# Gate values placed by two products of the rounded type, and weight halves made by a casting DMA

## Chip, cores and metric

The kernel runs on one core of a Trainium2 chip. The metric is the device time of one execution in microseconds; a kernel is timed by the median of several runs.

## What is computed

Two transformer blocks on one sequence of 256 positions of width 1024, all in float32. The change lies in the last part of the second block, a mixture of 16384 small experts (`peer_ffn`). For each position, eight heads score 2 x 128 keys, take the 16 best of each half, combine them into 256 candidates, take the 16 best of these, and turn their scores into 16 gates by a softmax. An expert's number is 128 i + j, where i comes from one half and j from the other. The block's output is the sum over the 128 picked experts of gate x gelu(u . x) x v.

```
sv, si = lax.top_k(s, PEER_TOPK)
cand_idx = (si[:, :, 0, :, None] * PEER_NKEYS + si[:, :, 1, None, :]).reshape(...)
best, pick = lax.top_k(cand, PEER_TOPK)
expert_idx = jnp.take_along_axis(cand_idx, pick, axis=-1)
gates = jax.nn.softmax(best, axis=-1)
...
u = expert_u[ic]
hval = jnp.einsum('cd,chkd->chk', xc, u).astype(jnp.float32)
a = (gc * jax.nn.gelu(hval, approximate=False)).astype(xc.dtype)
return jnp.einsum('chk,chkd->cd', a, expert_v[ic])
```

## The kernel before

**The dense form.** The kernel gathers nothing. It computes u . x for all 16384 experts, applies gelu, multiplies by a gate matrix that is zero wherever an expert was not picked, and multiplies by all of v. The matrix is `GT` [128, 128, 256]: j on the partitions, then i, then the position t. The first linear part (`linear(..., P, 8, evu)`) fills `GT` with gelu(u . x) in pairs of i; the last part (L1550, L1559) multiplies by v.

**Weights.** Each matrix product is done in three products of a rounded type (`float32r`, FR in the code), for which weights and inputs are split into a rounded half and a remainder. `unit()` makes one weight tile of 128 x 1024: SyncE issues the load of `raw` (L202), ScalarE writes the rounded half `whi` (L206), VectorE (or GpSimd, where `pool_k` is set) subtracts and writes `wlo` (L209). `raw`, `whi` and `wlo` have three buffers each; `take(2)` keeps two tiles ahead of the one in use. TensorE then runs 24 products of 256 columns with a tile, three (L231, L232, L233) for each of its eight 128 x 128 blocks. One tile of the first linear part serves one i.

**Gates.** `topk` finds i, j and the gate for each position on VectorE, in two rounds of 128 positions, and transposes them into `it["i"]`, `it["j"]`, `it["g"]` (tiles ti, tj, tg), so that a position's 128 picks lie along the partitions. When both rounds are done, `wstep()` starts: 64 steps of four positions each, run beside the first linear part. A step has two halves. `build` (VectorE, then ScalarE) writes two one-hot matrices per position: `oe`, which lies in `xres` (L1468), for i, and `oj` (L1469) for j, and ScalarE multiplies `oe` by the gate into `om` (L1471, one instruction per position). `place`, one step later, multiplies the two on TensorE (L1478, four products in plain float32, each 128 columns wide), which gives the position's 128 x 128 gate matrix in PSUM. What is there of gelu by then (the first `i1` values of i) is multiplied by it on VectorE (L1481), the rest of the gates is copied into `GT` by ScalarE (L1483). Where gelu comes later, `evu` writes it (L1454) or multiplies it in (L1457 on ScalarE and L1458 on VectorE). `oj` and `om` have two buffers each.

**Order.** `linear` calls `tick` after each tile; the steps run at a rate of 1.75 per pair of tiles, so most tiles are followed by one step. The instruction order on each engine is then settled by the tile framework when the program is built; an engine takes its instructions strictly in that order.

Of the kernel before, what the change touches and what calls it, by code (L numbers as in the profile page):

```python
# [8 lines left out]
FT = mybir.dt.float32  # L9
FR = mybir.dt.float32r  # L10
# [3 lines left out]
AF = mybir.ActivationFunctionType  # L14
OP = mybir.AluOpType
# [3 lines left out]
P = 128  # L19
S = 256  # L20
# [142 lines left out]
class Kernel:  # L163
    def __init__(self, ctx, tc, A, out):
        self.ctx, self.tc, self.A, self.out = ctx, tc, A, out
        self.nc = tc.nc
        nc = self.nc
        self.cst = ctx.enter_context(tc.tile_pool(name="cst", bufs=1))
        self.wp = ctx.enter_context(tc.tile_pool(name="wp", bufs=2))
        self.unit_i = 0  # L170
        self.ahead = []
        self.pos = 0
        self.bg = []
        self.pool_k = 0
        self.soon = []
        self.acc_bufs = 2
        self.vec = self.cst.tile([P, A["vec"].shape[1]], FT, name="vec")
        nc.sync.dma_start(self.vec, A["vec"])
        self.main = self.cst.tile([P, 3, P], FT, name="main")
        self.ident, self.ones, self.iota = (self.main[:, i, :] for i in range(3))  # L180
        self.eps = self.cst.tile([P, 3], FT, name="eps")
        for i, e in enumerate((EPS, LN_EPS, LNX_EPS)):
            nc.gpsimd.memset(self.eps[:, i:i + 1], e)
        self.mod = self.cst.tile([P, 48], FT, name="mod")
        self.junk = self.cst.tile([P, 1], FT, name="junk")
        self.hx = [self.cst.tile([P, 8, S + 2], FR, name=n) for n in ("hh", "hl")]
        self.hh, self.hl = (h[:, :, :S] for h in self.hx)
        self.r1 = self.cst.tile([P, 4], FT, name="r1")
        self.gm = self.cst.tile([P, 8], FT, name="gm")
        self.g2 = self.cst.tile([P, 8], FT, name="g2")  # L190
# [8 lines left out]
    def unit(self):  # L199
        nc = self.nc  # L200
        raw = self.raw()
        nc.sync.dma_start(raw, self.A["wts"][self.unit_i])  # L202
        self.unit_i += 1
        hi = self.wp.tile([P, 8, P], FR, name="whi", bufs=3)
        lo = self.wp.tile([P, 8, P], FR, name="wlo", bufs=3)
        nc.scalar.activation(hi, raw, AF.Copy)  # L206
        c = 8 - self.pool_k
        if c:
            nc.vector.tensor_tensor(lo[:, :c], raw[:, :c], hi[:, :c].bitcast(FT), op=OP.subtract)  # L209
        if c < 8:  # L210
            nc.gpsimd.tensor_tensor(lo[:, c:], raw[:, c:], hi[:, c:].bitcast(FT), op=OP.subtract)  # L211
        return hi, lo
# [1205 lines left out]
    def peer(self):  # L1418
        nc, tc = self.nc, self.tc
        V, SC, G, T = nc.vector, nc.scalar, nc.gpsimd, nc.tensor  # L1420
        x = self.xres
        with ExitStack() as es:
            pk = es.enter_context(tc.tile_pool(name="pk", bufs=1))
            it = {n: pk.tile([P, S], FT, name="t" + n) for n in ("i", "j", "g")}
            GT = pk.tile([P, P, S], FT, name="GT")
            with ExitStack() as e2:
                dp = e2.enter_context(tc.tile_pool(name="dp", bufs=1, space=bass.MemoryType.DRAM))
# [33 lines left out]
                io4 = self.iota[:, None, :].to_broadcast([P, 4, P])  # L1461

                def build(t0):
                    oj = pw.tile([P, 4, P], FT, name="oj")
                    om = pw.tile([P, 4, P], FT, name="om")
                    oe = wide[2 + t0 // 4 % 2].rearrange("p a (b c) -> p (a b) c", b=2)
                    z = slice(t0, t0 + 4)
                    V.tensor_tensor(oe, io4, it["i"][:, z, None].to_broadcast([P, 4, P]), op=OP.is_equal)  # L1468
                    V.tensor_tensor(oj, io4, it["j"][:, z, None].to_broadcast([P, 4, P]), op=OP.is_equal)  # L1469
                    for j in range(4):  # L1470
                        SC.activation(om[:, j, :], oe[:, j, :], AF.Copy, scale=it["g"][:, t0 + j:t0 + j + 1])  # L1471
                    return t0, oj, om

                def place(t0, oj, om):
                    i1 = st["u"]
                    wps = psum.tile([P, 4, P], FT, name="ax")
                    for j in range(4):
                        T.matmul(wps[:, j, :], oj[:, j, :], om[:, j, :], start=True, stop=True)  # L1478
                    z = slice(t0, t0 + 4)
                    if i1:  # L1480
                        V.tensor_tensor(Gv[:, z, :i1], Gv[:, z, :i1], wps[:, :, :i1], op=OP.mult)  # L1481
                    if i1 < P:
                        SC.activation(Gv[:, z, i1:], wps[:, :, i1:], AF.Copy)  # L1483
                    st["n"] = t0 + 4
# [12 lines left out]
                def start_w():  # L1497
                    for _ in top():
                        yield
                    self.pool_k = 0  # L1500
                    self.spawn(wstep(), 1.75)

                self.pool_k = 8
# [10 lines left out]
                                                     op=OP.subtract)  # L1514

                self.linear(psum, hh, hl, P, 8, evu, outer=True)
                self.drain()
                es5.close()
                po = e2.enter_context(tc.tile_pool(name="po", bufs=2))
# [59 lines left out]
    def topk(self, psum, qh, keys, scr, it, st):  # L1579
# [36 lines left out]
        for t in range(2):  # L1616
# [55 lines left out]
            T.transpose(tp[:, 1, :], res[:, 1].rearrange("p h k -> p (h k)"), self.ident)  # L1672
            T.transpose(tp[:, 2, :], e.rearrange("p h k -> p (h k)"), self.ident)
            z = slice(t * P, (t + 1) * P)
            for i, n in enumerate("ijg"):
                SC.activation(it[n][:, z], tp[:, i, :], AF.Copy)
            yield

    def build(self):
# [25 lines left out]
```

## Time and profile before

| what | value |
|---|---|
| median of three runs | 1557.8 us (1556.55 to 1558.47) |
| the profiled execution, its own time | 1556.54 us |
| its span, first to last instruction | 1554.8 us |
| share of the span in which TensorE is busy | 97% |
| VectorE, ScalarE, GpSimd | 73%, 54%, 22% |
| first product of a step, last product of a step | 923.2 us, 1185.3 us |
| data moved | 279.67 MB, mean 180 GB/s |

The page names TensorE as the engine that is nearly always at work, but a busy share is an average over stages. What matters for the change is the stretch from about 906 us, when the gates are found, to 1197 us, when the first linear part is over. In the rows below PE is a product on TensorE, PEld the weight load that goes with each product, DVE is VectorE, ACT ScalarE, POOL GpSimd, SP SyncE. A product's duration includes its way through the array, so two products overlap: the pace is read from the distance of their starts.

### The profile page before, as it was taken

What the parts mean: (1) busy time and instruction counts of PE and PEld (TensorE: products, weight loads), DVE (VectorE), ACT (ScalarE), POOL (GpSimd) and SP (SyncE); (2) the same over time, 40 slices, a digit from 0 to 9 for tenths busy, and PEclk for the clock granted to TensorE, in tenths of its full rate; (3) what the DMA queues carried; (4) which work ended last, traced back from release to release, by engine and by line L of the source; (5) the groups of instructions that cost most, each with busy time, mean ns of one, the idle gap of its engine ahead of it and who ended that gap; (6) DMA issues with size and microseconds to landing.
All of it is one profiled execution on the core that took longest, in us unless ns stands there. A gap on an engine that the chain in (4) does not pass through costs nothing.

```text
span 1554.8 us, 28988 instructions
## 1 busy us (share of the span) xinstructions
PE 1510.4 (97%) x11494; PEld 1409.9 (91%) x11494; DVE 1130.5 (73%) x1811; ACT 839.1 (54%) x1400; POOL 335.9 (22%) x301
## 2 busy tenths in 40 slices
PE   6898999999999999999999999999999999999998
PEld 5797889999999999999999999999999888888886
DVE  7789976787656677667689968889997555555555
ACT  4563334666644365544445457777775445454444
POOL 7614644325500100025790600000000000000000
PEclk9899999999999999999999999999999999999999
DMA  9445557476565644447456564444445665666664
GB/s 365 153 157 166 175 164 230 150 257 198 172 198 182 201 150 142 144 150 229 151 177 190 163 190 136 150 149 137 150 149 174 207 208 184 193 197 191 192 196 127
DMA packets 75449, 279.67 MB, mean 180 GB/s; under 512 B 8369, under 2 KB 9009, under 8 KB 73649
## 3 DMA queue, kind: packets, MB, share of 16 engines
q1 hardware_dynamic: 75312, 277.82, 56.1%
q8 instruction: 90, 1.47, 0.4%
q14 instruction: 47, 0.38, 0.1%
HBM read 275.69 MB, written 2.10 MB: 179 GB/s over the span
## 4 chain that ended last, share of the span: by engine, by line
PE 46%; DVE 2%; POOL 1%; issue 1%; ACT 0%; DVEq 0%
PE ax L1550 22%; PE mm L233 7%; PE mm L232 7%; PE mm L231 7%; PE ax L1478 4%; POOL wlo L211 1%; POOL GT L1627 0%; DVE GT L1659 0%; DVE GT L1566 0%; DVE GT L1657 0%; DVE wlo L209 0%; PE ax L1600 0%; DVE GT L1568 0%; DVE GT L1637 0%; DVE GT L1638 0%
## 5 line engine op out<-in xcount | busy, mean ns | idle before, releaser
L206 ACT ACTIVATE whi<-raw 128x1024 fp32r<-128x1024 f32 x453 | 478.6, 1058 | 535.8 <-PE mm L232 205.5
L209 DVE TENSOR_TENSOR wlo<-raw,whi 128x1024 fp32r<-128x1024 f32 (+2 forms) x413 | 496.3, 1204 | 265.0 <-ACT whi L206 264.4
L231 PE MATMUL mm<-hh,whi 128*128 128x256 f32 x1816 | 523.8, 288 | 3.7 <-ACT gate L581 2.5
L233 PE MATMUL mm<-hh,wlo 128*128 128x256 f32 x1816 | 514.9, 284 | 3.2 <-DVE wlo L209 2.3
L232 PE MATMUL mm<-hl,whi 128*128 128x256 f32 x1816 | 512.0, 282 | 1.1 <-DVE hl L1513 0.7
L231 PEld LDWEIGHTS mm<-hh,whi 128*128 128x128 f32 x1816 | 344.0, 189 | 9.5 <-issue 4.7
L233 PEld LDWEIGHTS mm<-hh,wlo 128*128 128x128 f32 x1816 | 344.8, 190 | 5.1 <-DVE wlo L209 2.7
L232 PEld LDWEIGHTS mm<-hl,whi 128*128 128x128 f32 x1816 | 345.2, 190 | 2.9 <-issue 1.4
L211 POOL TENSOR_TENSOR wlo<-raw,whi 128x256 fp32r<-128x256 f32 (+2 forms) x112 | 187.9, 1684 | 159.9 <-ACT whi L206 99.9
L1550 PE MATMUL ax<-whi,ah 128*128 128x512 f32 x504 | 155.6, 390 | 0.0
L1550 PE MATMUL ax<-whi,al 128*128 128x512 f32 x504 | 155.3, 389 | 0.0
L1550 PE MATMUL ax<-wlo,ah 128*128 128x512 f32 x504 | 155.1, 389 | 0.0
L1550 PEld LDWEIGHTS ax<-whi,al 128*128 128x128 f32 x504 | 94.6, 188 | 19.8
L1550 PEld LDWEIGHTS ax<-wlo,ah 128*128 128x128 f32 x504 | 94.6, 188 | 19.7
L1550 PEld LDWEIGHTS ax<-whi,ah 128*128 128x128 f32 x504 | 94.2, 188 | 19.2
L1471 ACT ACTIVATE om<-xres,tg 128x128 f32<-128x128 f32 x256 | 85.2, 391 | 1.0 <-DVE xres L1468 1.0
L233 PE MATMUL ax<-hh,wlo 128*128 128x258 f32 x256 | 72.9, 285 | 1.3 <-DVE wlo L209 1.3
L1481 DVE TENSOR_TENSOR GT<-GT,ax 128x208 f32<-128x208 f32 (+31 forms) x64 | 62.4, 974 | 16.1 <-PE ax L1478 15.9
L231 PE MATMUL ax<-hh,whi 128*128 128x258 f32 x256 | 72.7, 284 | 0.0
L232 PE MATMUL ax<-hl,whi 128*128 128x258 f32 x256 | 72.2, 282 | 0.0
L231 PE MATMUL mm<-fh,whi 128*128 128x256 f32 x256 | 72.1, 282 | 0.0
L232 PE MATMUL mm<-fl,whi 128*128 128x256 f32 x256 | 72.0, 281 | 0.0
(539 smaller groups left out, 2393.6 us busy)
## 6 DMA issues: line engine op xcount, KB each, us to landing
raw<-in_wts SPq DMA_DIRECT2D x453, 512.0 KB, 3.6
raw<-in_ada SPq DMA_DIRECT2D x24, 512.0 KB, 4.0
araw<-in_ada SPq DMA_DIRECT2D x8, 1024.0 KB, 7.9
w0r<-in_w SPq DMA_DIRECT2D x8, 576.0 KB, 8.9
araw<-in_ada SPq DMA_DIRECT2D x8, 512.0 KB, 4.8
x<-in_x SPq DMA_DIRECT2D x1, 1024.0 KB, 5.1
mb<-in_x SPq DMA_DIRECT2D x2, 512.0 KB, 5.3
selh<-in_att SPq DMA_DIRECT2D x1, 1024.0 KB, 5.9
```

The costliest lines, as they stand in the source:

```text
L206: nc.scalar.activation(hi, raw, AF.Copy)
L209: nc.vector.tensor_tensor(lo[:, :c], raw[:, :c], hi[:, :c].bitcast(FT), op=OP.subtract)
L211: nc.gpsimd.tensor_tensor(lo[:, c:], raw[:, c:], hi[:, c:].bitcast(FT), op=OP.subtract)
L231: mm(ps, wh, xh, start=start, stop=False, **kw)
L232: mm(ps, wh, xl, start=False, stop=False, **kw)
L233: mm(ps, wl, xh, start=False, stop=stop, **kw)
L1471: SC.activation(om[:, j, :], oe[:, j, :], AF.Copy, scale=it["g"][:, t0 + j:t0 + j + 1])
L1478: T.matmul(wps[:, j, :], oj[:, j, :], om[:, j, :], start=True, stop=True)
L1481: V.tensor_tensor(Gv[:, z, :i1], Gv[:, z, :i1], wps[:, :, :i1], op=OP.mult)
L1550: T.matmul(acc[t][c], a[:, u, z], w[:, c * 512:(c + 1) * 512], start=i + u == 0 and n == 0, stop=False)
```

## The change

Three things change together.

1. The gate is split like a weight: `it["h"]` is the gate in the rounded type, `it["l"]` the remainder, written by one more VectorE subtraction per round of `topk`.
2. `om` becomes [128, 2, 4, 128] in the rounded type, so ScalarE writes eight instructions per step instead of four, and `oj` is written in the rounded type. `place` runs two rounded products per position, summed in PSUM, instead of one in plain float32.
3. From the end of `topk` to the end of the first linear part (`self.cast`), `whi` isn't written by ScalarE from `raw`. GpSimd issues a second load of the same weights from memory, which rounds them on the way (the tile's type differs from the source's).

```diff
         hi = self.wp.tile([P, 8, P], FR, name="whi", bufs=3)
         lo = self.wp.tile([P, 8, P], FR, name="wlo", bufs=3)
-        nc.scalar.activation(hi, raw, AF.Copy)
+        if self.cast:
+            nc.gpsimd.dma_start(hi, self.A["wts"][self.unit_i - 1])
+        else:
+            nc.scalar.activation(hi, raw, AF.Copy)
...
                 def build(t0):
-                    oj = pw.tile([P, 4, P], FT, name="oj")
-                    om = pw.tile([P, 4, P], FT, name="om")
+                    oj = pw.tile([P, 4, P], FR, name="oj")
+                    om = pw.tile([P, 2, 4, P], FR, name="om")
...
-                    for j in range(4):
-                        SC.activation(om[:, j, :], oe[:, j, :], AF.Copy, scale=it["g"][:, t0 + j:t0 + j + 1])
+                    for n, part in enumerate("hl"):
+                        for j in range(4):
+                            SC.activation(om[:, n, j, :], oe[:, j, :], AF.Copy,
+                                          scale=it[part][:, t0 + j:t0 + j + 1].bitcast(FT))
...
                     for j in range(4):
-                        T.matmul(wps[:, j, :], oj[:, j, :], om[:, j, :], start=True, stop=True)
+                        for n in range(2):
+                            T.matmul(wps[:, j, :], oj[:, j, :], om[:, n, j, :], start=n == 0, stop=n == 1)
...
                     for _ in top():
                         yield
                     self.pool_k = 0
+                    self.cast = True
                     self.spawn(wstep(), 1.75)
...
                 self.linear(psum, hh, hl, P, 8, evu, outer=True)
+                self.cast = False
...
-            for i, n in enumerate("ijg"):
+            for i, n in enumerate("ijh"):
                 SC.activation(it[n][:, z], tp[:, i, :], AF.Copy)
+            V.tensor_tensor(it["l"][:, z], tp[:, 2, :], it["h"][:, z].bitcast(FT), op=OP.subtract)
```

The order on the engines moves too. VectorE, before, in the middle of the steps (two tiles, two steps; the name xres stands for `oe` in L1468 and for the piece of gelu that L1458 multiplies in):

```order
L209 TENSOR_TENSOR wlo<-raw,whi 128x1024
L1469 TENSOR_TENSOR oj<-main,tj 128x512
L1468 TENSOR_TENSOR xres<-main,ti 128x512
L1469 TENSOR_TENSOR oj<-main,tj 128x512
L1458 TENSOR_TENSOR GT<-GT,xres 128x2x84
L1481 TENSOR_TENSOR GT<-GT,ax 128x4x76
L209 TENSOR_TENSOR wlo<-raw,whi 128x1024
L1468 TENSOR_TENSOR xres<-main,ti 128x512
L1481 TENSOR_TENSOR GT<-GT,ax 128x4x76
```

VectorE at the same place after the change, where L213 is the line of `wlo`, L1472 of `oe`, L1473 of `oj`, L1462 of gelu's piece and L1488 of the product with the placed gates:

```order
L213 TENSOR_TENSOR wlo<-raw,whi 128x1024
L1472 TENSOR_TENSOR xres<-main,ti 128x512
L1462 TENSOR_TENSOR GT<-GT,xres 128x2x84
L1488 TENSOR_TENSOR GT<-GT,ax 128x4x76
L1473 TENSOR_TENSOR oj<-main,tj 128x512
L213 TENSOR_TENSOR wlo<-raw,whi 128x1024
L1472 TENSOR_TENSOR xres<-main,ti 128x512
L1488 TENSOR_TENSOR GT<-GT,ax 128x4x76
L1473 TENSOR_TENSOR oj<-main,tj 128x512
```

Each `wlo` now stands ahead of one `oe`, one product with the placed gates and one `oj`, in the same turn for every tile. ScalarE, before, at the same place:

```order
L1471 ACTIVATE om<-xres,tg 128x128 x4
L1483 ACTIVATE GT<-ax 128x4x52
L206 ACTIVATE whi<-raw 128x1024
L1471 ACTIVATE om<-xres,tg 128x128 x2
L1483 ACTIVATE GT<-ax 128x4x52
L1471 ACTIVATE om<-xres,tg 128x128 x2
L206 ACTIVATE whi<-raw 128x1024
```

ScalarE after the change; th and tl are the gate's two halves, L1490 the copy of placed gates:

```order
L1476 ACTIVATE om<-xres,th 128x128 x2
L1490 ACTIVATE GT<-ax 128x4x52
L1476 ACTIVATE om<-xres,th 128x128 x2
L1476 ACTIVATE om<-xres,tl 128x128 x4
L1476 ACTIVATE om<-xres,th 128x128 x2
L1490 ACTIVATE GT<-ax 128x4x52
L1476 ACTIVATE om<-xres,th 128x128 x2
L1476 ACTIVATE om<-xres,tl 128x128 x4
```

`whi` is gone from ScalarE, a step has eight `om` there, and the copy of an earlier step's gates stands behind the second of them. GpSimd, after its last `wlo` of `topk`, has this and nothing else:

```order
L215 TENSOR_TENSOR wlo<-raw,whi 128x1024 x4
L208 DMA whi<-in_wts 128x1024 x79
```

The 79 casting loads stand at the end of its queue, where before it had no work.

## Rows read from the trace of the kernel before

**Rows 1.** The page's head: span, busy time of each engine.

```profile
span 1554.8 us, 28988 instructions
...
PE 1510.4 (97%) x11494; PEld 1409.9 (91%) x11494; DVE 1130.5 (73%) x1811; ACT 839.1 (54%) x1400; POOL 335.9 (22%) x301
```

**Rows 2.** Busy time by stretch; then TensorE's granted clock, DMA share, GB/s.

```profile
core 0: us, PE busy (x) PEld busy (x) DVE busy (x) ACT busy (x) POOL busy (x), PEclk, DMA share, GB/s
906.00:1197.00 291.00, 291.00 (x2484) 290.99 (x2483) 244.26 (x308) 208.25 (x477) 0.00 (x0) 1.00 0.49 150
```

**Rows 3.** Waits of 906 to 1197 us: who for whom, total, times, longest.

```profile
ACT whi L206 <- PE mm L232: 41.8, 52, 1.8
ACT GT L1483 <- DVE GT L1481: 18.1, 39, 2.6
DVE wlo L209 <- ACT whi L206: 17.9, 18, 1.9
```

**Rows 4.** Instructions grouped, 906 to 1197 us: count, busy us, mean ns.

```profile
L209 DVE TENSOR_TENSOR wlo<-raw,whi 128x1024 fp32r<-128x1024 f32 x83 | 101.1, 1218 | 17.9 <-ACT whi L206 17.9
L206 ACT ACTIVATE whi<-raw 128x1024 fp32r<-128x1024 f32 x83 | 87.9, 1059 | 64.3 <-PE mm L232 41.8 <-issue 15.0 <-ACT om L1471 6.9
L1471 ACT ACTIVATE om<-xres,tg 128x128 f32<-128x128 f32 x248 | 82.6, 391 | 0.0
L1478 PE MATMUL ax<-om,oj 128*128 128x128 f32 x512 | 67.3, 274 | 0.0
L1478 PEld LDWEIGHTS ax<-om,oj 128*128 128x128 f32 x512 | 62.4, 191 | 0.0
L233 PEld LDWEIGHTS mm<-hh,wlo 128*128 128x128 f32 x656 | 123.9, 189 | 0.0
```

**Rows 5.** TensorE in order of time, from one step to the next.

```profile
1010.18 0.28 PE L233 MATMUL mm<-hh,wlo 128*128 128x256 f32 x1
1010.30 1.05 PE L1478 MATMUL ax<-om,oj 128*128 128x128 f32 x8
1011.11 0.36 PE L231 MATMUL mm<-hh,whi 128*128 128x256 f32 x1
1011.31 0.28 PE L232 MATMUL mm<-hl,whi 128*128 128x256 f32 x1
...
1013.92 0.28 PE L233 MATMUL mm<-hh,wlo 128*128 128x256 f32 x1
1014.04 1.05 PE L1478 MATMUL ax<-om,oj 128*128 128x128 f32 x8
```

**Rows 6.** Narrow and wide products in order of time: one column plain, 512 columns rounded.

```profile
169.19 1.95 PE L430 MATMUL ax<-main,acc 128*128 128x1 f32 x16
...
1541.65 0.39 PE L1559 MATMUL ax<-whi,al 128*128 128x512 f32 x1
1541.88 0.39 PE L1559 MATMUL ax<-wlo,ah 128*128 128x512 f32 x1
```

**Rows 7.** VectorE and ScalarE in order of time around one step.

```profile
1008.42 1.20 DVE L209 TENSOR_TENSOR wlo<-raw,whi 128x1024 fp32r<-128x1024 f32 x1
1009.55 0.67 DVE L1469 TENSOR_TENSOR oj<-main,tj 128x512 f32<-128x512 f32 x1
1010.15 0.67 DVE L1468 TENSOR_TENSOR xres<-main,ti 128x512 f32<-128x512 f32 x1
...
1012.07 0.33 DVE L1458 TENSOR_TENSOR GT<-GT,xres 128x168 f32<-128x168 f32 x1
1012.32 0.86 DVE L1481 TENSOR_TENSOR GT<-GT,ax 128x304 f32<-128x304 f32 x1
...
1011.92 1.27 ACT L1471 ACTIVATE om<-xres,tg 128x128 f32<-128x128 f32 x4
1013.21 0.56 ACT L1483 ACTIVATE GT<-ax 128x208 f32<-128x208 f32 x1
```

**Rows 8.** Weight loads and the DMA engines, 906 to 1186 us: count, KB, median us to landing.

```profile
DMA packets 11376, 41.69 MB, mean 149 GB/s; under 512 B 1264, under 2 KB 1264, under 8 KB 11349
...
raw<-in_wts SPq DMA_DIRECT2D x79, 512.0 KB, 3.6
```

**Rows 9.** The same for 311 to 350 us.

```profile
DMA packets 2729, 9.99 MB, mean 256 GB/s; under 512 B 300, under 2 KB 300, under 8 KB 2725
...
raw<-in_wts SPq DMA_DIRECT2D x13, 512.0 KB, 4.4
araw<-in_ada SPq DMA_DIRECT2D x6, 512.0 KB, 4.8
```

**Rows 10.** The same for 0 to 39 us.

```profile
DMA packets 2846, 14.22 MB, mean 365 GB/s; under 512 B 305, under 2 KB 561, under 8 KB 1713
...
raw<-in_wts SPq DMA_DIRECT2D x3, 512.0 KB, 7.1
```

**Rows 11.** VectorE in order of time, in and after the first round of `topk`.

```profile
841.28 0.29 DVE L1668 TENSOR_TENSOR GT<-GT 128x128 f32<-128x128 f32 x1
...
846.98 1.23 DVE L209 TENSOR_TENSOR wlo<-raw,whi 128x1024 fp32r<-128x1024 f32 x1 [1.62 <-ACT whi L206]
```

More of the change, by code (lines that the diff above doesn't have):

```diff
@@ L1423, in peer @@
             pk = es.enter_context(tc.tile_pool(name="pk", bufs=1))
-            it = {n: pk.tile([P, S], FT, name="t" + n) for n in ("i", "j", "g")}
+            it = {n: pk.tile([P, S], FR if n == "h" else FT, name="t" + n) for n in ("i", "j", "h", "l")}
             GT = pk.tile([P, P, S], FT, name="GT")
@@ L1516, in peer @@
                 self.linear(psum, hh, hl, P, 8, evu, outer=True)
+                self.cast = False
                 self.drain()
```

## Prediction

> **What bounds the kernel now.** I read the page's head first: TensorE is at work in 97% of the span [rows 1]. That says little of the stretch that the change touches, so I cut it out: from 906 to 1197 us TensorE has no idle time at all, its granted clock is 1.00 (the 2.4 GHz level), VectorE is busy for 244 us of 291, ScalarE for 208, and GpSimd does nothing [rows 2]. The waits of that stretch show no row with PE waiting for anybody. Those that are there are ScalarE's and VectorE's, and they are early rather than late: ScalarE waits 41.8 us in all for TensorE to let go of a `whi` buffer [rows 3]. So here an engine other than TensorE can only lose time: less work on ScalarE buys nothing, and the stretch gets shorter only if TensorE's own work does.
>
> That work, in order of time, is a cycle of 3.74 us, 1010.30 to 1014.04 us: one step and the 24 products of one tile [rows 5]. The step is eight records, since a plain float32 product of 128 columns shows as two. They take 1.05 us with 0.27 for one [rows 4, 5], so they start every (1.05 - 0.27) / 7 = 0.111 us, and a step costs 8 x 0.111 = 0.89 us. The tile's products take the other 2.85 us, 0.119 each.
>
> **The change on TensorE.** It removes 4 x 2 plain records per step and adds 4 x 2 rounded products: eight for eight, 512 for 512 in all [rows 4]. What a rounded product of 128 columns costs, the trace doesn't show; none is narrower than 256. Lower bound: 512 columns take 0.23 us from start to start [rows 6], 256 take 0.119, so a column costs 0.43 ns and the rest is 0.009: 128 columns would take 0.064 us if only the columns counted. Upper bound: a rounded product costs what a whole plain one does, 2 x 0.111 = 0.222 us. Nearest row: sixteen plain records of a single column need 1.95 us, with 0.25 for one that is (1.95 - 0.25) / 15 = 0.113 us each [rows 6]. With one column to stream, something else sets the pace, and each record has a weight load before it. That load lasts 191 ns in the step and 189 ns for a rounded tile [rows 4], so I take it to be equally dear for both types. The pace is then 0.111 to 0.119 us, and I take 0.115: 512 x 0.004 = 2 us more.
>
> The page "TensorE: Matmul & The Clock Gate" of the Trainium skill (section "LDWEIGHTS (loading the stationary operand)") gives a weight load's time as its columns over 1.2 GHz, an estimate of 107 ns for 128; the trace's 113 ns agrees. The same page ("Back-to-back issue gap") has columns / 2.4 + 2.5 ns for an isolated warm product, an estimate of 56 ns here: by it the sum would lose 512 x 0.055 = 28 us instead of gaining 2.
>
> **ScalarE.** Four `om` more per step at (1.27 - 0.39) / 3 = 0.293 us each [rows 7] add 64 x 4 x 0.293 = 75 us; 79 `whi` of 1.06 us [rows 4] are gone, 84 us. Its total stays about 200 of 291 us and is hidden under TensorE. What grows is the way from `oe` to the step's products: eight `om` last 7 x 0.293 + 0.39 = 2.44 us instead of 1.27. VectorE's two further subtractions in `topk` are 128 x 128, about 0.29 us each [rows 11]; the first stands where VectorE waits 1.62 us for ScalarE anyway [rows 11], the second ahead of tiles that are two cycles early. I take zero; without that cover it is 0.6.
>
> **The casting load.** Before, `whi` took ScalarE 1.06 us from the moment its buffer was free. Now the moment is the same, the end of the products of the tile three earlier, but a transfer follows. `wlo` waits for it, and in VectorE's strict order `oe`, the product with the placed gates and `oj` wait behind `wlo`; ScalarE's copy of these gates, and six of the eight `om` behind it, wait for VectorE. How late may it land? Set 0 where tile k's products end. TensorE then runs step 0 (0.89), tile k+1 (2.85), step 1, tile k+2, step 2, and tile k+3 from 3 x 0.89 + 2 x 2.85 = 8.37; step 3 starts at 11.22. Counted by the order after the change, the gates behind `wlo` of k+3 are step 1's, and the `om` behind their copy are step 3's. From landing to the last of these: `wlo` 1.13, `oe` 0.60, gelu's piece 0.25, the gates' product 0.86, the copy 0.46, six `om` 5 x 0.293 + 0.39 = 1.86 (the starts of [rows 7], for the copy 0.56 less an overlap of 0.10), and some 0.15 for the handoffs: 5.3 us. So a landing up to 11.2 - 5.3 = 5.9 us after release costs nothing. `wlo` alone would allow 8.37 - 1.2 = 7.1.
>
> When does it land? 512 KB take 3.6 us beside a mean of 149 GB/s [rows 8], 4.4 to 4.8 beside 256 GB/s [rows 9] and 7.1 beside 365 GB/s [rows 10]. The change adds 79 x 0.524 = 41 MB to 41.7 MB in the same 280 us [rows 8]: 297 GB/s. Between the last two that is 4.8 + 41 / 109 x 2.3 = 5.7 us. These are SyncE's loads; no row has one from GpSimd, nor one that changes the type, so the bounds are 3.6 and 7.1, with nothing known above if rounding slows the engines. 5.7 is just inside 5.9. Each us above costs about 79 / 3 = 26 us: the release that a late tile waits for is three tiles back, so lateness is paid once in three tiles. For 5.7 with some scatter I put the mean lateness at 0.1 us, 3 us.
>
> The page "DMA: Bandwidth & Descriptors" of the Trainium skill ("Specifications") has the first byte of a load from GpSimd at about 1 us and from SyncE at 0.6; no run here shows it yet. By it an idle landing would be 3.6 + 0.4 = 4.0 us, and the sum would not change unless the engines are loaded too.
>
> **Sum.** 1556.5 us (the profiled execution; its span is 1554.8) + 2 (narrow products) + 0 (ScalarE, `topk`) + 3 (late landings) = 1561.5. The median of the runs shown is 1.3 above the profiled one, so 1563.
>
> **Rivals.**
> - Hidden altogether: landings under 5.5 us and narrow products at 0.111. For it: [rows 9] show 4.8 under a mean not far below. Time: 1558, no change.
> - Faster: the narrow product costs its columns only. Against it is the single-column row; for it, that both of that row's types are plain. At 0.064 a step is 0.38 us shorter, 64 x 0.38 = 24 us. VectorE's turn of one tile and one step, 1.13 + 0.60 + 0.25 + 0.86 + 0.60 = 3.4 us [rows 7], would then meet TensorE's 3.36 about half-way through, as the gates' product grows with i1; so I put 12 of the 24, 1546. It decides as soon as the pace is under 0.105 us (512 x 0.006 = 3 us). This rival's rule is the gap formula of the Trainium skill's page "TensorE: Matmul & The Clock Gate" ("Back-to-back issue gap").
> - Late landings: over 6.2 us, because two streams meet on the same 16 engines or the rounding is slow. At 7.1 it is 26 x 1.2 = 31 us, 1589; at 6.2, 8 us.
> - Narrow products at the whole plain price, 0.222: 512 x 0.111 = 57 us, 1615. For it is only that nothing in the trace excludes it.
>
> **How the numbers follow.** Chances: my forecast 0.35 (own range 1559 to 1568), hidden 0.25, late 0.18, faster 0.14, whole price 0.08. No change means within 0.2%, about 3 us, which is what a measurement of this kernel can tell. "Same" takes the hidden case and 0.05 of mine, 0.30; "slower" is 0.30 + 0.18 + 0.08 = 0.56; "faster" 0.14. The range of 8 in 10 leaves out the whole price (0.08), the late case beyond 7.5 us (0.03) and the faster case below 1550 (0.09): 1550 to 1602.
>
> **What would show it.** Right: 512 records of the new products, starting every 0.11 to 0.12 us, so the step still takes about 0.9 us; PE rows free of waits, or with a few us on `wlo` and `om`; `whi` loads landing 5 to 6 us after issue, DMA near 300 GB/s; VectorE waiting for a DMA where it waited for ScalarE. Wrong: starts 0.06 or 0.22 us apart; a landing of 4 us; or one of 8 with the 16 engines full, PE waiting at every tile, and perhaps a granted clock that no longer stays at the upper level.

## The result, and the profile after

The changed kernel takes 1568.45 us (median of 9 runs, 1565.3 to 1572.32) against 1558.95 for the kernel before in the same comparison (9 runs, 1556.55 to 1563.21). The ratio is 1.0056, with a 95% interval of 1.0045 to 1.0067: it is slower by some 9 us. The page's head answers to [rows 1]:

```profile
span 1568.1 us, 29276 instructions
...
PE 1517.4 (97%) x11494; PEld 1413.6 (90%) x11494; DVE 1129.4 (72%) x1813; ACT 828.0 (53%) x1577; POOL 378.9 (24%) x380
```

TensorE runs as many instructions as before, but is busy for 7 us more and the span is 13.3 us longer. Part of that is no effect of the change: the profiled execution of before lies 2.4 us under its median, that of after 1.4 us over. So I read the time from marks on TensorE's line that both kernels have: the first transpose of the gates in `topk`, the first and the last step, the first product of the last part.

```profile
845.82 0.27 PE L1671 MATMUL ax<-main,GT 128*128 128x128 f32 x1
923.20 0.27 PE L1478 MATMUL ax<-om,oj 128*128 128x128 f32 x1
1184.50 0.27 PE L1478 MATMUL ax<-om,oj 128*128 128x128 f32 x1
1196.80 0.39 PE L1550 MATMUL ax<-whi,ah 128*128 128x512 f32 x1
```

Those are before, and these after:

```profile
848.36 0.27 PE L1680 MATMUL ax<-main,GT 128*128 128x128 f32 x1
927.22 0.34 PE L1485 MATMUL ax<-om,oj 128*128 128x128 f32 x2
1194.74 0.34 PE L1485 MATMUL ax<-om,oj 128*128 128x128 f32 x2
1209.37 0.47 PE L1559 MATMUL ax<-whi,ah 128*128 128x512 f32 x1 [1.49 <-DMA whi<-in_wts]
```

Differences of the starts give a table that the experiments below extend (us):

| kernel | gates to first step | first to last step | last step to last part | sum |
|---|---|---|---|---|
| before | 77.38 | 261.30 | 12.30 | 350.98 |
| after | 78.86 | 267.52 | 14.63 | 361.01 |

The 2.5 us by which the first mark is later lie ahead of everything that was changed. The stretch itself is 10.0 us longer, and the three columns say where: 1.5, 6.2 and 2.3 us. In the stretch as a whole (columns as in [rows 2]) TensorE is no longer always busy:

```profile
906.00:1209.00 303.00, 298.31 (x2506) 295.81 (x2504) 243.44 (x308) 195.92 (x646) 42.07 (x79) 1.00 0.88 280
```

The granted clock is 1.00 (the 2.4 GHz level) as before, so the clock is no cause. TensorE's waits of 906 to 1210 us, where [rows 3] had none:

```profile
PE mm L237 <- DVE wlo L213: 3.4, 7, 0.9
PE ax L1559 <- DMA whi<-in_wts: 1.5, 1, 1.5
```

Only seven products wait for `wlo`, and one for a load. The rows understate the price: the wait of 0.81 us shown below puts its product off by 0.97 us and the next one by 1.07.

The price of the gates' products is in the groups (count, busy us, mean ns) and on TensorE's line; they answer to [rows 4] and [rows 5]:

```profile
L1485 PE MATMUL ax<-om,oj 128*128 128x128 f32 x512 | 65.5, 270 | 0.1
L1485 PEld LDWEIGHTS ax<-om,oj 128*128 128x128 f32 x512 | 63.3, 191 | 0.4 <-ACT om L1476 0.2
L208 POOL DMA_DIRECT2D whi<-in_wts x79 | 42.1, 533 | 279.1 <-PE mm L237 137.4 <-PE mm L236 61.2 <-DVE wlo L213 26.6
```

```profile
1010.85 1.00 PE L1485 MATMUL ax<-om,oj 128*128 128x128 f32 x8
1011.69 0.33 PE L235 MATMUL mm<-hh,whi 128*128 128x256 f32 x1
1011.86 0.28 PE L236 MATMUL mm<-hl,whi 128*128 128x256 f32 x1
...
1014.60 0.45 PE L1485 MATMUL ax<-om,oj 128*128 128x128 f32 x3
```

512 records again, a weight load of 191 ns again. Read product by product, the second starts 0.06 us after the first and the others every 0.11 us. From the step's start to the second product behind it takes 1.01 us, exactly as before (1010.30 to 1011.31). The cycle is 3.75 us instead of 3.74.

The loads (906 to 1200 us) answer to [rows 8]:

```profile
DMA packets 22591, 82.60 MB, mean 281 GB/s; under 512 B 2497, under 2 KB 2497, under 8 KB 22561
...
raw<-in_wts SPq DMA_DIRECT2D x80, 512.0 KB, 4.5
whi<-in_wts POOLq DMA_DIRECT2D x77, 512.0 KB, 4.9
```

A median of 4.9 us is harmless in a step's cycle. But read in windows of 1 us the casting loads spread from 3.8 to 8.1 us; before, `raw` had no landing over 4.9. The worst one, in order of time from its issue to the stall:

```profile
1040.31 0.53 POOL L208 DMA_DIRECT2D whi<-in_wts  x1 [2.32 <-PE mm L236]
1048.48 1.22 DVE L213 TENSOR_TENSOR wlo<-raw,whi 128x1024 fp32r<-128x1024 f32 x1 [3.38 <-issue]
1048.67 0.28 PE L236 MATMUL mm<-hl,whi 128*128 128x256 f32 x1
1049.76 0.39 PE L237 MATMUL mm<-hh,wlo 128*128 128x256 f32 x1 [0.81 <-DVE wlo L213]
```

The window in which it was issued names both loads:

```profile
whi<-in_wts POOLq DMA_DIRECT2D x1, 512.0 KB, 8.1
raw<-in_wts SPq DMA_DIRECT2D x1, 512.0 KB, 7.8
```

The third product of the tile was due at 1048.79. `wlo` takes 1.22 us, so the load was allowed 1048.79 - 1.22 - 1040.31 = 7.3 us, and it took 8.1. VectorE's row puts the wait down to "issue", since the profile shows no releaser for it; the start of `wlo` is the landing to within a tenth.

Not all of the loss is of this kind. Behind that landing the lateness stays in the other engines:

```profile
1052.48 1.51 PE L1485 MATMUL ax<-om,oj 128*128 128x128 f32 x8
...
1066.95 0.67 DVE L1473 TENSOR_TENSOR oj<-main,tj 128x512 fp32r<-128x512 f32 x1
1067.55 1.21 DVE L213 TENSOR_TENSOR wlo<-raw,whi 128x1024 fp32r<-128x1024 f32 x1
1068.82 0.39 PE L237 MATMUL mm<-hh,wlo 128*128 128x256 f32 x1 [0.19 <-DVE wlo L213]
```

The step at 1052.48 takes 1.51 us instead of 1.00: its products go out at the pace at which ScalarE writes `om`, in gaps too short to be listed as waits. Three steps are stretched like this (1052, 1060 and 1142 us), 1.1 us in all. And the wait at 1068.82 is not behind a late load. The load of that tile, issued at 1060.81, landed after 5.2 us, at 1066.02; `wlo` began at 1067.55, when VectorE was through with `oj`. VectorE's turn, from one `wlo` to the next, lasts 3.5 to 4.1 us there, on average no less than TensorE's 3.75, so it does not catch up, and the next tile without a step finds it late. Of the seven waits for `wlo`, three are of this kind (1069, 1159 and 1188 us); they cost 1.7 us.

### The profile page after: what moved, and what is told of

It is laid out like the page before. It is cut to its first block, busy times and chain, and to the rows that moved or that the text cites. A ratio compares the mean times of both kernels' runs of the same rounds, so it can differ in the third digit from the quotient of the medians.

```text
span 1568.1 us, 29276 instructions
## 1 busy us (share of the span) xinstructions
PE 1517.4 (97%) x11494; PEld 1413.6 (90%) x11494; DVE 1129.4 (72%) x1813; ACT 828.0 (53%) x1577; POOL 378.9 (24%) x380
## 4 chain that ended last, share of the span: by engine, by line
PE 29%; DVE 7%; issue 7%; DMA 3%; ACT 3%; POOL 1%; POOLq 0%; DVEq 0%
PE ax L1559 22%; DMA whi<-in_wts 3%; PE mm L237 2%; PE mm L235 2%; PE mm L236 2%; ACT om L1476 2%; DVE GT L1488 2%; DVE wlo L213 1%; DVE xres L1472 1%; PE ax L1485 1%; ACT GT L1490 1%; DVE oj L1473 1%; POOL wlo L215 0%; DVE GT L1462 0%; DVE GT L1646 0%
## 5 line engine op out<-in xcount | busy, mean ns | idle before, releaser
L213 DVE TENSOR_TENSOR wlo<-raw,whi 128x1024 fp32r<-128x1024 f32 (+2 forms) x413 | 495.5, 1202 | 294.3 <-ACT whi L210 244.9
L210 ACT ACTIVATE whi<-raw 128x1024 fp32r<-128x1024 f32 x374 | 395.0, 1058 | 483.5 <-PE mm L236 161.8
L208 POOL DMA_DIRECT2D whi<-in_wts x79 | 42.1, 533 | 279.1 <-PE mm L237 137.4
L1476 ACT ACTIVATE om<-xres,th 128x128 fp32r<-128x128 f32 x256 | 86.5, 389 | 3.0 <-PE ax L1485 1.8
L1476 ACT ACTIVATE om<-xres,tl 128x128 fp32r<-128x128 f32 x256 | 81.3, 391 | 0.0
L1490 ACT ACTIVATE GT<-ax 128x304 f32<-128x304 f32 (+31 forms) x64 | 30.1, 471 | 82.1 <-DVE GT L1488 82.1
L237 PE MATMUL mm<-fh,wlo 128*128 128x256 f32 x256 | 72.9, 285 | 0.0
```

The lines of the kernel that those rows point to most:

```text
L208: nc.gpsimd.dma_start(hi, self.A["wts"][self.unit_i - 1])
L237: mm(ps, wl, xh, start=False, stop=stop, **kw)
L1476: SC.activation(om[:, n, j, :], oe[:, j, :], AF.Copy, scale=it[part][:, t0 + j:t0 + j + 1].bitcast(FT))
```

## Experiments

Theory A: the loss is made by casting loads that land late. Rival B: it is made by the products and the longer chain on ScalarE. Rival C: two streams slow the stretch as a whole, in proportion to their traffic. All ratios are to the kernel before, timed beside each run.

### The two parts apart

Products alone: in the changed kernel the line that turns the casting load on is taken out.

```diff
                     self.pool_k = 0
-                    self.cast = True
                     self.spawn(wstep(), 1.75)
```

> Only the products change: the high halves of the weights are made by ScalarE again, as before, and the gate values are placed by two rounded products. Theory A (the loss is made by casting loads that land late): the waits of the products on the low halves go, raw loads land within 3.4 to 5 us again, and the time is that of before within about 2 us, 1557 to 1561. Rival B (the loss is made by the products or the longer chain of copies on ScalarE): 1565 to 1570. ScalarE is the danger for both: 208 us busy in the stretch of before plus 75 us of new copies is about 283 of 291 us, so a queue on ScalarE may show, seen as waits of TensorE on copies of lines 1476 or 210, and would speak for neither A nor B about the changed kernel.

Load alone: the gates as before, with the casting load. Of the edits that take the gates back the one at the products is shown.

```diff
...
-                        for n in range(2):
-                            T.matmul(wps[:, j, :], oj[:, j, :], om[:, n, j, :], start=n == 0, stop=n == 1)
+                        T.matmul(wps[:, j, :], oj[:, j, :], om[:, j, :], start=True, stop=True)
...
```

> Only the load changes: one plain product per position as before, the high halves by the casting load. Theory A: the same late landings (some loads 6 to 8 us) and the same waits as in the changed kernel, +7 to +10 us, 1566 to 1569. Rival B: 1558 to 1560, as before.

The load alone gives 1568.55 us, 1.0045 (1.0032 to 1.0058), as A said. TensorE waits for one thing, nine times:

```profile
PE mm L237 <- DVE wlo L213: 6.7, 9, 1.5
```

The products alone give 1612.24 us, 1.0335 (1.032 to 1.035). That is far outside both ranges. The expectation had named a queue on ScalarE as a danger, by its busy time; what shows is a new wait, and the casting load covers it in the changed kernel. VectorE and ScalarE in order of time, through one turn of 5.17 us (1051.44 to 1056.61):

```profile
1050.53 0.88 DVE L1488 TENSOR_TENSOR GT<-GT,ax 128x312 f32<-128x312 f32 x1
...
1051.44 0.52 ACT L1490 ACTIVATE GT<-ax 128x200 f32<-128x200 f32 x1 [1.21 <-DVE GT L1488]
...
1052.01 1.27 ACT L1476 ACTIVATE om<-xres,tl 128x128 fp32r<-128x128 f32 x4
1053.18 1.05 ACT L210 ACTIVATE whi<-raw 128x1024 fp32r<-128x1024 f32 x1
...
1054.26 1.23 DVE L213 TENSOR_TENSOR wlo<-raw,whi 128x1024 fp32r<-128x1024 f32 x1 [0.25 <-ACT whi L210]
...
1055.68 0.90 DVE L1488 TENSOR_TENSOR GT<-GT,ax 128x320 f32<-128x320 f32 x1
...
1056.61 0.53 ACT L1490 ACTIVATE GT<-ax 128x192 f32<-128x192 f32 x1 [0.67 <-DVE GT L1488]
```

This is a ring through two engines that each keep their order: the gates' product on VectorE, the copy that waits for it, the low `om`, `whi`, `wlo` behind `whi`, the gates' product again. It is longer than TensorE's cycle of 3.75 us although ScalarE is busy for only 248 of 306 us (930 to 1236 us). With the casting load, `whi` leaves the ring. So the two parts aren't independent: the products need the load, and bring nothing themselves.

To price the products without that ring, the low half goes to GpSimd, which has nothing else to do there:

```diff
...
+                    for j in range(4):
+                        SC.activation(om[:, 0, j, :], oe[:, j, :], AF.Copy, scale=it["h"][:, t0 + j:t0 + j + 1].bitcast(FT))
+                    G.tensor_tensor(om[:, 1], oe, it["l"][:, z, None].to_broadcast([P, 4, P]), op=OP.mult)
...
```

> The two rounded products without the casting load and without the longer chain on ScalarE: high halves of the weights by ScalarE, as before, the high gate part by four ScalarE copies, as before, the low gate part by one GpSimd multiplication for four positions. If the load alone makes the loss and the two rounded products cost what the plain one did (0.111 us each), the time is that of before within 2 us, 1558 to 1562. If the 50 us of the run with the products alone were made by the products and not by ScalarE's chain of eight copies, it is far above, over 1590. A slow GpSimd multiplication (over some 2.5 us, or VectorE slowed beside it) would show as waits of TensorE on om from GpSimd.

1562.51 us, 1.0022 (1.0013 to 1.0031), slightly outside "within 2 us". In the marks its steps take 262.15 us, 0.85 more than before, with a cycle of 3.75 to 3.76 and no wait of TensorE inside the steps. So two rounded products per position cost 0.85 us in the whole stretch. By the marks the kernel is 3.4 us longer than before; the other 2.5 us lie outside the steps (1.5 of them are lost in `topk`, from 859 to 863 us of its own time, where a product waits 0.84 us for `wlo` from GpSimd), and I can't tie them to the edit.

### How late, and where

A fourth buffer for the high halves, beside the load alone, lets a load go out a tile earlier:

```diff
...
+        if self.px and self.unit_i % 4 == 0 and self.unit_i < self.A["wts"].shape[0] - self.px_end:
+            hi = self.px.tile([P, 8, P], FR, name="whx", bufs=1)
+        else:
+            hi = self.wp.tile([P, 8, P], FR, name="whi", bufs=3)
...
```

> The load alone, with a fourth buffer for the high halves in the stretch (every fourth tile from a buffer of its own), so that a load can be issued one tile, 3.7 us, earlier. Theory A: a landing of 8 us is hidden, the waits on the low halves go but for the first tiles, and the time is 1558 to 1562. Rival C (both streams together slow the stretch as a whole, whatever the slack): as the load alone, 1566 to 1569.

1562.97 us, 1.002 (1.0007 to 1.0033), a little above A's range: 5.6 us of the load's 8.2 are back, though the rate of transfer is no lower (284 GB/s against 279, 906 to 1197 us) and landings of up to 8.0 us are still there. The steps take 262.15 us, 0.85 more than before and 4.8 less than with three buffers. C falls. TensorE's waits that are left lie at the two ends (the last part and the first tiles), but for the third, where a step at 1051 us waits for `om` behind a landing of 8.0 us:

```profile
PE ax L1562 <- DMA whi<-in_wts: 1.8, 1, 1.8
PE mm L241 <- DVE wlo L217: 0.9, 1, 0.9
PE ax L1486 <- ACT om L1479: 0.3, 1, 0.3
```

What is special at the ends, and at every eighth tile in between, is that no step follows the tile. The next experiment moves these bare tiles, with the load alone:

```diff
-                    self.spawn(wstep(), 1.75)
+                    self.spawn(wstep(), 2.0)
```

> The casting load alone with plain products, but a step of the gates on every tile, where the changed kernel leaves every eighth tile without one; the 15 tiles left come bare at the end. If loads land late because a tile without a step asks for its two loads after 2.9 us and not 3.7 (some 367 GB/s), then the tiles with steps show no landing above 6 us and no wait, and the 15 bare tiles show landings of 7 to 8 us and a wait on nearly each, 0.2 to 1 us: in all 1566 to 1575. If the late landings come from something else (instruction loads, a slow engine now and then), they and the waits are spread over the stretch as before, and the time is 1566 to 1569.

1569.12 us, 1.0057 (1.0044 to 1.0069), within the first branch's range and just above the second's; the trace decides (its execution lies 6.3 us over the median, 4.4 of them ahead of the gates' mark). While every tile has a step, 230 us long, both streams run at full rate and cost TensorE nothing:

```profile
930.00:1160.00 230.00, 230.00 (x1970) 230.00 (x1970) 208.37 (x276) 113.02 (x367) 32.19 (x61) 1.00 0.89 283
```

In the bare tiles behind them (1164 to 1204 us) TensorE is busy for 33.3 of 40 us, and waits for the load and for `wlo`:

```profile
PE mm L235 <- DMA whi<-in_wts: 3.4, 3, 1.9
PE mm L237 <- DVE wlo L213: 3.3, 4, 0.9
```

The arithmetic is that of the slack. From the release of a buffer to the tile that needs it lie two tiles and their steps; two bare tiles are 2 x 2.85 us, and a landing may take 5.70 + 0.24 - 1.22 = 4.7 us, which is less than the median of 4.9.

The casting load for every other tile halves its traffic, with the changed kernel's products and with plain ones:

```diff
-        if self.cast:
+        if self.cast and self.unit_i % 2:
```

> The changed kernel with the casting load for every other tile only, the other tiles' high halves by ScalarE. Theory A with a threshold: the streams together move a quarter less, landings stay below some 5.5 us, nearly no wait is left, 1558 to 1561. Rival C (a loss in proportion to the casting loads): half of the loss stays, about 1563.

> Plain products with the casting load on every other tile. Theory A: streams a quarter less, few landings above 5.5 us, no long chain on ScalarE: 1559 to 1562. If the half-cast run with rounded products lost its 20 us to the mixed load and not to ScalarE's eight copies, this one loses 10 us or more too.

Both miss. With the rounded products it takes 1580.19 us, 1.0127 (1.0112 to 1.0143): every other tile has `whi` in ScalarE's ring again, and TensorE waits for `wlo` (7.1 us), `oj` (3.1) and `om` (1.8). With plain products it takes 1567.34 us, 1.0051 (1.0037 to 1.0064), no better than the whole stream (by its marks, in the table below, 2.6 us better). Its steps lose 4.2 us, 4.0 of them in three places, behind loads that landed after 6.7, 8.2 and 8.1 us; the median is 4.9. So late landings aren't a matter of the mean rate, which is 214 GB/s here (906 to 1190 us): neither my threshold nor proportion holds. What one looks like, busy share of the 16 DMA engines and GB/s in 40 slices of 1040 to 1047 us:

```profile
DMA  9778989989888994343211100100000000009907
GB/s 304 281 281 304 421 304 398 281 304 328 351 328 328 398 421 187 140 140 117 94 70 47 47 23 23 47 23 23 23 23 23 23 23 0 0 0 94 164 23 257
```

From 1043 us on the rate falls in stages to 23 GB/s, which is one engine's share of the 365 GB/s in [rows 10] (365 / 16 = 23). For some 1.7 us nearly nothing but a single engine is at work: in the trace's packet records ten packets of 4 KB follow one another from 1044.22 to 1045.84 us, in turn from SyncE's queue and from GpSimd's. These two loads are late because one engine is behind, not because sixteen are full.

In the runs with the whole stream the other engines go on with the next loads, so their rate doesn't show this. But each load reports its end in sixteen parts, as many as there are engines, and the landing is the last. In the load alone, of the load issued at 1042.13 us fifteen parts are done after 4.7 us and the last after 8.0. In the changed kernel's worst load, the one of 1040.31 us, thirteen are done after 5.2 us and the others after 5.6, 7.0 and 8.1. The Trainium skill's page "DMA: Bandwidth & Descriptors" (section "Latency and other measured facts") has two of the engines as usually slower than the rest when GpSimd issues, and calls its reason a guess; that agrees in kind, but no view here tells which engine it was.

### What the products would have to cost

One rounded product per position instead of two:

```diff
-                        for n in range(2):
-                            T.matmul(wps[:, j, :], oj[:, j, :], om[:, n, j, :], start=n == 0, stop=n == 1)
+                        T.matmul(wps[:, j, :], oj[:, j, :], om[:, 0, j, :], start=True, stop=True)
```

> The changed kernel with one rounded product per position; the product with the low half of the value is left out, its four copies on ScalarE are still made. A price bound by the weights' fetch (0.111 us for a product) gives 4 records and 0.445 us less in a step, a cycle of 3.31 us; of the 28 us in 64 steps the two streams, which then ask for 13% more in the same time, take some back: 1545 to 1562. If one rounded product cost as much as the plain one's two records, the cycle stays at 3.75 and the time at 1568.

1562.79 us, 1.0023 (1.0007 to 1.0039), just above the top of the range. TensorE's quiet cycle (a step and a tile without a wait) is 3.28 us, so the saving on TensorE is there, 0.47 us a step or 30 us in all; 14.9 us of waits on `wlo` (22 of them) and 3.7 on the load, with what each costs besides, take back 24 of it. Most of that is no longer a landing: from the first step on, of 25 products that come over 0.15 us late for `wlo`, 16 have a `wlo` that began right behind other work of VectorE.

Next, bfloat16 for both matrices, with the gate split into two bfloat16 parts; then the same with the fourth buffer:

```diff
...
-                    oj = pw.tile([P, 4, P], FR, name="oj")
-                    om = pw.tile([P, 2, 4, P], FR, name="om")
+                    oj = pw.tile([P, 4, P], BF, name="oj")
+                    om = pw.tile([P, 2, 4, P], BF, name="om")
...
```

> The changed kernel with bfloat16 for the one-hot matrix and for both gate parts (the value split into two bfloat16 parts). If the narrow product is bound by its weights' fetch and bfloat16 fetches faster, the eight products of a step fall from 0.89 us to between 0.45 and 0.6 us, 18 to 28 us of TensorE in 64 steps; the two load streams then ask for some 9% more in the same time, so that the late landings grow and give some of it back: 1545 to 1560. If bfloat16 has the same pace, 1568 as the changed kernel.

> As the bfloat16 version, with a fourth buffer for the high halves. Theory A: late landings are hidden for one tile more, so 4 to 8 us under the run without the buffer. Rival C: no difference.

The groups of the first (906 to 1190 us) show the weight load halved:

```profile
L1485 PE MATMUL ax<-om,oj 128*128 128x128 bf16 x512 | 39.7, 220 | 0.0
L1485 PEld LDWEIGHTS <-oj 128*128 128x128 bf16 x512 | 28.7, 98 | 2.6
```

Its step is a record of 0.62 us for eight products of 0.22, a pace of (0.62 - 0.22) / 7 = 0.057 us where the rounded one has 0.11, and the quiet cycle is 3.34 to 3.35 us. Still it takes 1562.07 us, 1.0016 (1.0007 to 1.0025), above its range: 12.3 us of waits on `wlo`, 23 of them. Here too VectorE is the next limit. Behind a late landing it takes 15.3 us for four turns, 3.83 each, against TensorE's 3.35:

```profile
1107.21 1.23 DVE L213 TENSOR_TENSOR wlo<-raw,whi 128x1024 fp32r<-128x1024 f32 x1 [2.08 <-DMA whi<-in_wts]
...
1122.51 1.22 DVE L213 TENSOR_TENSOR wlo<-raw,whi 128x1024 fp32r<-128x1024 f32 x1
```

From the first step on, of 37 products that come over 0.15 us late for `wlo`, 31 have a `wlo` that began right behind other work of VectorE, and 6 one that began at a landing. With the fourth buffer it takes 1552.93 us, 0.9951 (0.9938 to 0.9965), faster than both kernels. Nine us for the buffer are somewhat more than A's 4 to 8. What is left for TensorE to wait for (906 to 1200 us):

```profile
PE ax L1489 <- DVE oj L1477: 5.3, 9, 1.3
PE mm L241 <- DVE wlo L217: 2.1, 3, 0.8
PE ax L1489 <- ACT om L1480: 1.3, 3, 0.6
```

bfloat16 without the casting load at all, the low half by GpSimd:

> bfloat16 products without the casting load: weight halves by ScalarE, high gate part by ScalarE, low gate part by one GpSimd multiplication. If bfloat16 is faster and GpSimd keeps up, 1558 less 18 to 28 us: 1530 to 1542, faster than both kernels; if ScalarE's or VectorE's chain around a step binds first, in between; if bfloat16 has the same pace, 1558 to 1562.

1553.76 us, 0.9961 (0.9948 to 0.9975): faster than both, but by the middle branch, not the first. VectorE is nearly full, and TensorE waits 5.8 us for `oj` (906 to 1190 us: 284.00 us, then TensorE, weight loads, VectorE):

```profile
906.00:1190.00 284.00, 273.31 (x2497) 265.99 (x2497) 270.20 (x313) 198.24 (x479) 94.03 (x62) 1.00 0.50 155
```

Last, the gates' matrices two steps ahead and the last part's tiles by ScalarE, on the bfloat16 version with the fourth buffer:

```diff
...
-                        if len(q) == 1:
+                        if len(q) == 2:
...
-        if self.cast:
+        if self.cast and self.unit_i <= self.A["wts"].shape[0] - 128:
...
```

> The bfloat16 version with a fourth buffer, and two more edits: the gates' matrices are made two steps ahead of their products instead of one, and the tiles of the last part are rounded by ScalarE again. The 5.3 us of waits on the one-hot matrix and the 1.8 us at the first product of the last part should go: 1543 to 1549, against 1552.9 without the two edits. If these waits only move to the low halves, no change.

1552.89 us, 0.9951 (0.9937 to 0.9964): no change. The way from the last step to the last part falls from 13.20 to 10.39 us and the waits on `oj` are gone, but 6.4 us of waits on `wlo` stand in their place (2.1 before the edits), and the first step comes 7 us later after the gates (85.61 us against 78.61), some of it in waits on `wlo` and `whi` ahead of 906 us. That last part I didn't follow further.

The marks of the runs that bear on the cause (us, as in the first table):

| kernel | gates to first step | first to last step | last step to last part | sum |
|---|---|---|---|---|
| load alone | 78.73 | 266.99 | 15.43 | 361.15 |
| load alone, fourth buffer | 78.59 | 262.15 | 14.80 | 355.54 |
| products alone, low half by GpSimd | 79.21 | 262.15 | 13.00 | 354.36 |
| load on every other tile, plain products | 78.72 | 265.48 | 14.34 | 358.54 |
| bfloat16 | 78.79 | 259.97 | 13.20 | 351.96 |
| bfloat16, fourth buffer | 78.61 | 249.04 | 13.20 | 340.85 |

The profiled execution of the last row lies 4.3 us under that kernel's median, so its sum may be low.

## Why the prediction was right in its mechanism and short in its size

**TensorE.** The forecast of 0.115 us for a narrow rounded product was nearly right: it is 0.11 in the step, and the term of +2 us is 0.85 by the products priced apart. The rival "column-bound" fell, and so did the whole plain price. The deciding row was rightly the weight load, equal in both types (191 ns). bfloat16 shows the other side: halve the load (98 ns) and the pace falls to 0.057 (the streamed matrix changed type with it; no run separates the two). By the page "TensorE: Matmul & The Clock Gate" of the Trainium skill ("Back-to-back issue gap") the estimate was 56 ns; the trace agrees for bfloat16 and not for the rounded type.

**ScalarE and `topk` at zero.** Nearly right, in the changed kernel: ScalarE is busy for 196 us, and no listed wait of TensorE leads to `om`. But the three stretched steps (1.1 us) went at ScalarE's pace, and the load alone has none: all its 64 steps take the same time. And the cover that I named, TensorE's own time, wasn't the one that mattered. The +75 and -84 us don't cancel as sums; they cancel since `whi` leaves the ring. Without the casting load the same products cost 52 us at a busy share that looks harmless.

**Late landings: the term that was mis-sized.** I put 3 us; the runs show about three times that. The load alone loses 8.2 us by the medians (10.2 by the marks of its profile), the changed kernel 9.5 (10.0), of which the products make 0.85. By its marks the changed kernel loses 1.3 us at the first casting loads, 5.4 in stalls between the steps (6.2 less 0.85) and 2.3 on the way to the last part; another 0.2 lies in `topk`. Of the 5.4, three waits behind loads of 6.4, 7.7 and 8.1 us make 2.6, the stretched steps behind the last two of these 1.1, and the three waits for a VectorE that had not caught up 1.7. Two steps of the working failed, and in opposite senses.
- "Between the last two that is ... 5.7 us": the mean rate came out at 281 GB/s, not 297, and the median at 4.9 us. Interpolating on the mean rate was the wrong tool altogether. The loads that cost something between the steps are the tail of 6.4 to 8.2 us, which half the stream has too.
- "a landing up to ... 5.9 us after release costs nothing": this was worked out for three tiles with steps, where a single late load in fact has 7.3 us (the chain to the third step's `om` that made it 5.9 does bind, but later: in the changed kernel a landing of 6.0 us, issued at 1165.46, leaves all steps at 1.00 us, and behind those of 7.7 and 8.1 us that step takes 1.37 and 1.51; with four `om`, and a step on each tile, landings of up to 6.4 us pass without a wait). A bare tile takes 0.89 us of slack away, and at both ends of the stretch there are no steps: 4.7 us are allowed, and an ordinary landing is late.

By its own rule a median of 4.9 us under a limit of 5.9 would have cost nothing, as in the rival "hidden altogether". That the forecast of 1563 us came near the 1568 measured is in part luck: the working put the landing too late and the limit too high for the tiles that count. It also had VectorE's turn at 3.4 us, and only in a rival: at 3.5 to 4.1, as long as TensorE's cycle, it carries a lateness on instead of making it up.

So the rival "late landings over 6.2" was right in its kind for some loads and wrong in putting all loads there; "hidden altogether" holds for 230 us of the run with a step on each tile. The loss is paid in single stalls (waits of 0.2 to 1.5 us in the changed kernel), not as 26 us for each us of lateness.

**Where the hoped gain went.** There was none on TensorE to lose: eight records for eight at the same pace. What stays open is why one DMA engine falls behind. Many of the long loads go out at the end of a bare tile, 2.85 us after the one before (the one of 8.1 us above is such a case), but not all do, and most loads at that place land in time.

The traces name a rival that no run tests. By their packet records the DMA engines also carry fetches of instructions, 16 KB each, 0.9 to 2.1 us long in the changed kernel, about every 15 us. In the changed kernel each of the six casting loads of over 6 us between the first and the last step has such a fetch within 4.9 us of its issue, and of the 44 loads without one none took over 5.5 us. With the load alone it is 7 of 9 late loads, with every other tile 2 of 4 (plain products) and 0 of 4 (rounded, where no casting load had one). So a fetch often goes with a late load, but it is not always there, and 22 loads of the changed kernel had one and landed within 6 us. No run moves the fetches, and whether they are the cause isn't shown.

## What to carry to other kernels

Don't price a narrow product by its columns: look whether its weight load changes too, since at 128 columns that set the pace here. A transfer in place of a copy has to be judged by its worst landing against the smallest slack, at the ends of the loop and in the iterations that lack the side work, not by a median against a mean cycle; a buffer more was the cheapest cure here. Ask too whether the engine behind the transfer can catch up: if its turn is as long as the cycle, one late landing is carried on for many turns. And an engine busy for 80% of the time can still set the cycle, if its strict order and another's close a ring: add up the ring, not the busy time.

## What the runs showed of the hardware that was not expected

- float32r fetches 128 columns of weights in 191 ns, as plain float32 does; bfloat16 in 98 ns, and 512 narrow products then start every 0.057 us instead of 0.11. The Trainium skill's page "TensorE: Matmul & The Clock Gate" ("Weight-path perf modes — Fast Weight Load (FWL) and DoubleRow") says that the fast load is on for 128 weights when the type is not float32; the trace agrees for bfloat16, and float32r behaves as float32 here.
- A late load can be the work of a single DMA engine: 23 GB/s for some 1.7 us at the end of two loads of 512 KB, with the other engines idle; or fifteen of sixteen parts done after 4.7 us and the last after 8.0.
- The casting load costs GpSimd 0.53 us to issue, and its bytes take the DMA engines no longer than SyncE's: 41.7% of their time for 39.85 MB against 45.5% for 42.34 MB (906 to 1200 us).
- GpSimd's multiplication for the low half takes 1.18 us in the mean with the rounded type (930 to 1180 us of that run). VectorE's `oj`, beside which it runs at times, takes 0.83 us in the mean where it took 0.69 before; its median stays at 0.68, and the longest is 1.43.
